# Four gate tiles in the attention heads' buffers, and the first output projection started with heads 0 to 3

## The chip, the core and the metric

The kernel runs on one core of one Trainium2 chip. The core has a matrix engine (TensorE, in the profile PE, with its weight loads listed as PEld), a vector engine (VectorE, DVE), an activation engine (ScalarE, ACT), a general engine (GpSimd, POOL) and a synchronising engine (SyncE, SP). In this kernel SP and ACT also issue the transfers (DMA) between the chip's memory and the core's on-chip memory (SBUF). Matmuls write into accumulators (PSUM), which here are eight banks of 128 x 512 f32: three called `acc`, two `s`, two `pt` and one `po`. The metric is the device time of one execution, in microseconds (us). The profiler's trace is of one execution; its span is a little shorter than the time of that execution.

## What is computed

The reference is two layers of a decoder trunk over 1024 rows of 1024 columns. Layer 0 is dilated window attention, layer 1 a gated linear recurrence, and each layer also attends to 256 memory rows. Around every mixer stands the same frame:

```
h = rms_norm(x, norm_gain[l])
cols = h @ w_in_a[j]
mix = dilated_mixer(cols[..., :3 * A_QKV], cos, sin, q_gain_a[j], k_gain_a[j])
gate = cols[..., 3 * A_QKV + MEM_WIDTH:]
...
y = jnp.concatenate([mix, mem_out], axis=-1) * jax.nn.silu(gate)
x = x + y @ w_out
```

`mix` has 1024 columns (8 heads of 128) and `mem_out` 512, so `y` has 1536 columns, and so has `gate`. The change lies at the seam between the last columns of layer 0's gate and layer 0's product `y @ w_out`.

## The kernel before

**Precision.** Every large product is done as three matmuls on f32r halves: both operands are split into a high and a low part, and high x high, high x low and low x high are added up in one accumulator. A weight piece (512 KB) is loaded into one of two `raw` buffers (line 195, issued by SP), ACT copies its high part (`wh`, line 166 through `copy`), DVE makes the low part (`wl`, line 212). `ahead(n)` prepares pieces up to n beyond the one in use, in the order of a list, `plan`; `rooms` says which pool each piece of the first output projection goes to.

**The order of the instructions** is not written out by hand: the program is traced, and a planner orders each engine's instructions by its own timeline of when their inputs will be ready; earlier program text has priority. Each engine then runs its list in that order. `tc.issue_after(ins)` makes the instructions traced inside it that run on the engine of `ins` stand behind `ins`; transfers issued by SP are not bound by it.

**The last stretch of layer 0.** `project_tiles` (line 229) computes 512 columns for eight tiles of 128 rows, two tiles at a time, 24 matmuls of 128 x 512 a tile (lines 252 to 254). The last attention group (`Q, g` = 1, 0: heads 4 to 7, window 128) projects k, v, q and attends tile by tile; `attend` for the last tile (line 922, with `merge`, line 901) is left over, and is run inside the gate projection that follows. It reads two `os` tiles of the pool `gs` (two buffers of 2 KB a partition), which lines 898 and 918 fill and use up, and its result goes to `o_scr` in the chip's memory (line 920).

**The gate projection** `gate_chunk(1, ...)` (line 504) computes the gate columns of heads 4 to 7. Its `each(m, ps)` runs once a tile: ACT takes tanh of the accumulator (line 500), DVE multiplies it on (line 501), after which the accumulator is free, and the tile is stored to `gate_scr` by a transfer that ACT issues (line 517). The tile buffer comes from the heads' pool `ap_` (name `qn`, two buffers) for m < 2 and from `gs` (`os`) for the rest. After tile 1 `between()` runs the last `attend`, closes the attention's pools (`s1`, `sa`) and opens, in `begin_out_a`, the pools of the output projection over their memory. After the tanh of tiles 3, 5 and 7 stand `ahead(4)`, `ahead(7)` and `ahead(10)`.

**The first output projection** `out_proj("out_a", ..., by_tile=True)` (line 570) multiplies `y` by `w_out_a`. The 1536 columns are taken in three blocks of 512, `b0` = 8 (the memory heads), 0 (heads 0 to 3) and 4 (heads 4 to 7), in the order of `FIRST`. A step is one `(b0, m)`: 24 matmuls (lines 632 to 634). Tiles 0 and 1 go block by block (steps (8,0), (8,1), (0,0), (0,1), (4,0), (4,1)), tiles 2 to 7 tile by tile. For every step `load_a` (line 716) loads the mixer's output `ol` and the gate `gt`, and `y_a` (line 741) multiplies them (line 744). For blocks 0 and 4 `transposed_split` follows: four transposes on PE (line 294), high part on ACT (line 166), low part on DVE (line 273). For block 8 the operands lie transposed in memory already: ACT copies the high part and DVE makes the low part (line 749), with no work on PE. `begin()` loads and makes the first two steps while the gate's last two tiles are projected; their `gt` lies in a buffer of its own (`spare`), later ones in `gs`. The two sums of tile 0 are in `acc`, those of tile 1 in `s`.

Of the kernel before, what the change touches and what calls it, by code (L numbers as in the profile page):

```python
# [46 lines left out]
NT = S // 128  # L47
# [8 lines left out]
SQB = 1  # L56
MGP = ((0,),(1,),(),())
MG1 = (2, 3)
FIRST = (8, 0, 4)
GATE_A, GATE_B = 9 * 1024 + 512, 3 * 1024 + 512  # L60


# [55 lines left out]
def trunk_kernel(ctx, tc, x, mem, pos, norm_gain, w_in_a, q_gain_a, k_gain_a, qk_gain_t, w_out_a,  # L118
# [10 lines left out]
    gs = ctx.enter_context(tc.tile_pool(name="gs", bufs=2))  # L129
# [99 lines left out]
    def ahead(n):  # L229

        while at_piece[1] < min(at_piece[0] + n, len(plan)):
            ready[at_piece[1]] = piece(*plan[at_piece[1]][1:])
            at_piece[1] += 1
# [201 lines left out]
    def rows(scr, g, m):  # L435

        r0, st = tile_rows(g, m)
        return scr[r0:r0 + 127 * st + 1:st, :]
# [45 lines left out]
    def sequence_rows(scr, m):  # L484


        return scr[m * 128:(m + 1) * 128].rearrange("(l e) c -> e l c", e=8)
# [11 lines left out]
    def twice_silu(dst, src):  # L499
        tanh = A.activation(dst, src, AF.Tanh, scale=0.5).ins  # L500
        V.scalar_tensor_tensor(dst, dst, 1.0, src, op0=OP.add, op1=OP.mult)  # L501
        return tanh

    def gate_chunk(c, by_residue, between=None, room=None, end=None):


        splits = {3: 4, 5: 7, 7: 10}

        def each(m, ps):
            pool, name = room if room and m < 2 else (gs, "os")  # L510
            sg = pool.tile([128, 4, 128], F32, name=name)[:].rearrange("p h d -> p (h d)")
            tanh = twice_silu(sg, ps)
            scr = gate_scr[:, c * 512:(c + 1) * 512]
            if by_residue:
                SQ.dma_start(rows(scr, 2, m), sg)
            else:
                SQ.dma_start(sequence_rows(scr, m), sg)
            if between and m == 1:
                between()
            if between and m in splits:  # L520

                with tc.issue_after(tanh):
                    ahead(splits[m])

        project_tiles(("gate", c), lhs_natural, each, end=end)
# [44 lines left out]
    def out_proj(key, load, load_x, y_T, x1, finish, pool, before, by_tile=False):  # L570

        steps = [(b0, m) for b0 in FIRST for m in range(NT)]
        if by_tile:
            steps = [s for s in steps if s[1] < 2] + [(b0, m) for m in range(2, NT) for b0 in FIRST]
        loaded, made, W, sums = {}, {}, {}, {}

        def weights(b0):  # L580
            p = take((key, b0), 4)
            W[b0] = [p[0:2], p[2:4]]

        def fetch(i):
            if i < len(steps):
                loaded[i], last = load(steps[i][1], steps[i][0])
                xm = i - XL if not by_tile and XL <= i < NT + XL else None
                if by_tile and steps[i][0] == FIRST[-1]:
                    xm = steps[i][1]
                if xm is not None:  # L590
                    with tc.issue_after(last.ins):
                        load_x(xm)

        def make(i):
            if i < len(steps):
                hi = pool.tile([128, 4, 128], F32R, name="yhi", bufs=LEAD + 1)
                lo = pool.tile([128, 4, 128], F32R, name="ylo", bufs=LEAD + 1)
                y_T(steps[i][1], steps[i][0], loaded.pop(i), hi, lo)
                made[i] = hi, lo

        def begin():
            for i in range(LEAD):
                fetch(i)
            for i in range(LEAD):
                make(i)
            before()

        def rest():
            fetch(LEAD)
            later = None  # L610
            for i, (b0, m) in enumerate(steps):
                if m == 0:
                    weights(b0)
                fetch(i + LEAD + 1)
                make(i + LEAD)
                if later:
                    later()
                    later = None
                hi, lo = made.pop(i)
                if m == 1 and not by_tile:  # L620
                    ahead(2)
                first, end = (b0 == FIRST[0], b0 == FIRST[-1]) if by_tile else (True, True)
                if first:
                    pool_, name = (pS, "s") if by_tile and m == 1 else (pp, "acc")
                    sums[m] = [pool_.tile([128, 512], F32, name=name) for _ in range(2)]
                pss = sums[m]
                last = i == len(steps) - 1 and key == "out_b"
                for kp, ch in ((0, 0), (1, 0), (0, 1), (1, 1)) if last else ((0, 0), (0, 1), (1, 0), (1, 1)):
                    wh, wl = W[b0][kp][ch]
                    for j in range(2):  # L630
                        k = 2 * kp + j
                        T.matmul(pss[ch][:], hi[:, k, :], wh[:, j, :], start=first and k == 0, stop=False)  # L632
                        T.matmul(pss[ch][:], hi[:, k, :], wl[:, j, :], start=False, stop=False)  # L633
                        T.matmul(pss[ch][:], lo[:, k, :], wh[:, j, :], start=False, stop=end and k == 3)  # L634
                    if by_tile and i == 1 and kp == 1:
                        ahead(7 + ch)
                    if m == NT - 1:
                        ahead(min(4, 2 + 2 * kp + ch) if by_tile else 3 + 2 * kp + ch)
                for ch, ps in enumerate(pss) if end else ():
                    xs = x1[m][:, ch * 512:(ch + 1) * 512]  # L640
                    V.tensor_tensor(xs, xs, ps[:], op=OP.add)
                if b0 == FIRST[-1]:
                    later = finish(m)
            if later:
                later()

        return begin, rest
# [18 lines left out]
            plan_chunk((n, Q, g), w_in_a, i * 3072 + g * 1024 + Q * 512, order=None if g else ROLLED)  # L666
    plan_chunk(("gate", 1), w_in_a, GATE_A + 512)

    def plan_out(key, w):
        for b0 in FIRST:  # L670
            for kp in (0, 2):
                for ch in range(2):
                    plan_chunk((key, b0), w, ch * 512, (b0 + kp) * 128, 256)

    plan_out("out_a", w_out_a)

    def plan_gate(i):
        plan_slice(("gate_b", i), w_in_b, GATE_B + i * 128)
# [16 lines left out]
            plan_chunk(("vb", 4), w_in_b, 2048 + 512)  # L695
    for i in gate_order[2]:
        plan_gate(i)
    plan_out("out_b", w_out_b)

    wide = ExitStack()  # L700


    s2, out_a = ExitStack(), []

    def begin_out_a(s2):
# [10 lines left out]
        def load_a(m, b0):  # L716
            r = slice(m * 128, (m + 1) * 128)
            o = op.tile([128, 512], F32, name="ol", bufs=2)

            if m < 2 and b0 == 8:  # L720
                if not spare:
                    spare.append(op.tile([128, D], F32, name="xn", bufs=1))
                gt = spare[0][:, m * 512:(m + 1) * 512]
            else:
                gt = gs.tile([128, 4, 128], F32, name="os")[:].rearrange("p h d -> p (h d)")
            if b0 == 8:
                for t, scr in ((o[:], om_scr), (gt, gatem_scr)):
                    last = LQ.dma_start(t.rearrange("p (k t) -> p k t", k=4), scr[:, r].rearrange("(k p) t -> p k t", p=128))
            else:
                LQ.dma_start(o[:], o_scr[r, 0, b0 * 128:b0 * 128 + 512])  # L730
                last = LQ.dma_start(gt, gate_scr[r, b0 * 128:b0 * 128 + 512])
            return (o, gt), last
# [31 lines left out]
    with ExitStack() as sa:  # L764
# [9 lines left out]
        with ExitStack() as s0:  # L774
# [3 lines left out]
            for m in range(NT):  # L778
                xt = ipool.tile([128, D], F32, name="xt")
                first = Y.dma_start(xt[:], rows(x, 2, m))  # L780
# [28 lines left out]
            rest, parts = 2.0 * math.pi, []  # L809
            while rest > 0:  # L810
                e = 2.0 ** (math.floor(math.log2(rest)) - 6)
                c = math.floor(rest / e) * e
# [46 lines left out]
            def spill_v(m, ps):  # L859
# [9 lines left out]
                    after=lambda hp: gate_mem(MG1[hp], mp[1], "qn"))  # L869
        sm.close()  # L870

        with ExitStack() as s1:
            vring = s1.enter_context(tc.tile_pool(name="vring", bufs=8))
            at_ = s1.enter_context(tc.tile_pool(name="attn", bufs=2))
            ap_ = s1.enter_context(tc.tile_pool(name="heads", bufs=2))
# [100 lines left out]
            for Q, g in group_order:  # L976
# [41 lines left out]
                end = (lambda i: ahead(min(3 + i, WR))) if final else None  # L1018
# [4 lines left out]
                project_tiles(("q", Q, g), lhs, each_q, order, end)  # L1023
                last = lambda: attend(Q, g, *waiting.pop(), kT, kl, vv)
                if final:
                    def between():
                        last()
                        s1.close()
                        sa.close()
                        out_a.append(begin_out_a(s2))  # L1030

                    def to_out(i):
                        if i == 0:
                            out_a[0][0]()

                    gate_chunk(1, False, between, (ap_, "qn"), to_out)
                else:
                    last()

# [4 lines left out]
    with ExitStack() as sb:  # L1044
# [257 lines left out]
        with ExitStack() as s7:  # L1302
# [25 lines left out]
            def load_x(m):  # L1328
                LQ.dma_start(x1[m], x1_scr[m * 128:(m + 1) * 128, :])
# [62 lines left out]
```

## Time and profile before

| | us |
|---|---|
| time, median of 3 runs (lowest to highest) | 2167.69 (2166.01 to 2167.97) |
| the profiled execution, its own time | 2167.61 |
| span of its trace | 2165.5 |
| TensorE busy in the span | 2137.0 |
| first matmul of gate tile 5 | 1247.73 |
| last matmul of the gate projection starts | 1265.56 |
| first matmul of the first output projection | 1265.79 |
| first matmul of its third step, (0,0) | 1290.76 |

Times inside the span count from its start. Three kinds of answers of the trace are used below. A list of waits has one line for each pair of a waiting operation and the one that released it, with the total, the count and the longest wait. A table of stretches has, for each, its length, every engine's busy time with its number of instructions, the granted clock of TensorE as a share of full speed, the share of time in which the DMA engines were busy, and GB/s. A timeline has the start, the length, the engine, the line, the operation, output and input, the shape and the count; in brackets stands how long the engine was idle before it and what it waited for. Matmuls overlap in it: what one costs in a stream is the distance between two starts.

### The profile page before, as it was taken

The page shows a single profiled execution, that of the slowest core. Times are in us where ns is not written, and L with a number is a line of the kernel's source. Part 1 is how long each engine was busy: PE and PEld are TensorE (multiplying, and loading weights), DVE is VectorE, ACT ScalarE, POOL GpSimd, SP SyncE. Part 2 cuts the span into 40 slices and gives each one's busy share as a digit, 9 for nine tenths or more (in the row PEclk, how much of TensorE's full clock was granted, in tenths as well). Part 3 has the DMA queues.
Part 4 walks back from the last instruction along what each step waited for, and adds up shares of the span by engine and source line. Part 5 has one row for each costly group of instructions (what it writes and reads, how often), then busy time and mean ns, then how long its engine had stood idle before and what let it go on. Part 6 is the DMA issues. An engine that isn't in the chain of part 4 may idle for free.

```text
span 2165.5 us, 29606 instructions
## 1 busy us (share of the span) xinstructions
PE 2137.0 (99%) x11273; PEld 1816.9 (84%) x11273; DVE 1060.8 (49%) x2403; ACT 730.0 (34%) x1507; POOL 370.9 (17%) x600
## 2 busy tenths in 40 slices
PE   8999999999999999999999979999999999999999
PEld 6888888888888888888888868888888888888887
DVE  6755323425414314425725744434557772776543
ACT  4545323424324324324423432233523222232211
POOL 1013212313403203302312000012200000000221
PEclk9999999999999999999999989999999999999999
DMA  6543211121222121122311475431211212113633
GB/s 200 140 138 72 46 51 56 51 69 41 60 67 56 48 64 47 33 69 58 107 47 52 126 231 163 136 106 44 88 35 50 64 54 59 49 50 98 233 119 115
DMA packets 181004, 183.49 MB, mean 85 GB/s; under 512 B 49008, under 2 KB 117760, under 8 KB 180864
## 3 DMA queue, kind: packets, MB, share of 16 engines
q1 hardware_dynamic: 116592, 138.48, 21.2%
q10 hardware_dynamic: 64272, 43.13, 7.0%
q8 instruction: 89, 1.46, 0.3%
q14 instruction: 51, 0.42, 0.1%
HBM read 138.45 MB, written 43.12 MB: 84 GB/s over the span
## 4 chain that ended last, share of the span: by engine, by line
PE 96%; DMA 2%; DVE 1%; ACT 0%; issue 0%; SPq 0%; POOL 0%; ACTq 0%; DVEq 0%
PE acc L252 16%; PE acc L253 16%; PE acc L254 16%; PE acc L536 5%; PE acc L537 5%; PE acc L538 5%; PE acc L632 4%; PE acc L633 4%; PE acc L634 4%; PE po L965 3%; PE pt L311 2%; PE s L946 2%; PE s L1147 1%; PE pt L1147 1%; PE pt L959 1%; DMA raw<-in_w_out_a_dram 1%
## 5 line engine op out<-in xcount | busy, mean ns | idle before, releaser
L252 PE MATMUL acc<-wh,hhi 128*128 128x512 f32 x1440 | 563.7, 395 | 4.6 <-DVE os L501 3.5
L254 PE MATMUL acc<-wh,hlo 128*128 128x512 f32 x1440 | 566.0, 395 | 0.0
L253 PE MATMUL acc<-wl,hhi 128*128 128x512 f32 x1440 | 565.7, 393 | 0.0
L175 POOL TENSOR_TENSOR rr<-rv,nhalf 128x4 f32<-128x4 f32 (+1 forms) x150 | 148.2, 988 | 1386.9 <-DVE rv L173 1361.2
L212 DVE TENSOR_TENSOR wl<-raw,wh 128x1024 fp32r<-128x1024 f32 x152 | 188.5, 1242 | 383.1 <-ACT wh L166 381.3
L252 PEld LDWEIGHTS acc<-wh,hhi 128*128 128x128 f32 x1440 | 271.5, 189 | 58.6 <-DVE os L501 3.7
L253 PEld LDWEIGHTS acc<-wl,hhi 128*128 128x128 f32 x1440 | 271.3, 188 | 53.6 <-DVE wl L212 0.4
L254 PEld LDWEIGHTS acc<-wh,hlo 128*128 128x128 f32 x1440 | 271.0, 188 | 53.5
L166 ACT ACTIVATE wh<-raw 128x1024 fp32r<-128x1024 f32 x152 | 160.9, 1059 | 192.3 <-PE acc L254 55.2
L538 PE MATMUL acc<-hhi,wl 128*128 128x512 f32 x512 | 203.8, 398 | 0.0
L537 PE MATMUL acc<-hlo,wh 128*128 128x512 f32 x512 | 203.6, 398 | 0.0
L536 PE MATMUL acc<-hhi,wh 128*128 128x512 f32 x512 | 202.9, 396 | 0.0
L302 DVE TENSOR_REDUCE ss<-sq 128x4 f32<-128x512 f32 x116 | 79.3, 684 | 144.1 <-ACT sq L300 144.0
L632 PE MATMUL acc<-wh,yhi 128*128 128x512 f32 x360 | 144.0, 402 | 4.6 <-DVE os L501 3.5
L633 PE MATMUL acc<-wl,yhi 128*128 128x512 f32 x360 | 142.3, 395 | 0.0
L634 PE MATMUL acc<-wh,ylo 128*128 128x512 f32 x360 | 139.9, 395 | 0.0
L300 ACT ACTIVATE sq<-acc 128x512 f32<-128x512 f32 x116 | 68.9, 594 | 181.1 <-PE acc L254 177.0
L305 DVE TENSOR_TENSOR qn<-acc,rr 128x512 f32<-128x512 f32 x116 | 79.7, 688 | 92.9 <-PE pt L311 50.6
L954 ACT ACTIVATE pa<-pa,st 128x128 f32<-128x128 f32 (+1 forms) x192 | 84.5, 442 | 99.4 <-DVE st L952 92.0
L537 PEld LDWEIGHTS acc<-hlo,wh 128*128 128x128 f32 x512 | 96.3, 188 | 17.9
L536 PEld LDWEIGHTS acc<-hhi,wh 128*128 128x128 f32 x512 | 96.3, 188 | 17.7
L538 PEld LDWEIGHTS acc<-hhi,wl 128*128 128x128 f32 x512 | 96.3, 188 | 17.5
(241 smaller groups left out, 3195.8 us busy)
## 6 DMA issues: line engine op xcount, KB each, us to landing
raw<-in_w_in_a_dram SPq DMA_DIRECT2D x88, 512.0 KB
raw<-in_w_in_b_dram SPq DMA_DIRECT2D x40, 512.0 KB
o_scr<-os ACTq DMA_DIRECT2D x48, 256.0 KB
raw<-in_w_mem_kv_dram SPq DMA_DIRECT2D x16, 512.0 KB
os<-o_scr SPq DMA_DIRECT2D x32, 256.0 KB
raw<-in_w_out_a_dram SPq DMA_DIRECT2D x12, 512.0 KB
raw<-in_w_out_b_dram SPq DMA_DIRECT2D x12, 512.0 KB
gt<-gateb_scr SPq DMA_DIRECT2D x24, 256.0 KB
```

What stands on the lines that cost most here:

```text
L166: A.activation(dst, src, AF.Copy)
L175: G.tensor_tensor(r[:], v[:], nhalf[:, :n], op=OP.pow)
L212: W_LO.tensor_tensor(lo[:], raw[:], hi[:].bitcast(F32), op=OP.subtract)
L252: T.matmul(ps, hi, wh[:, j, :], start=at == 0, stop=False)
L253: T.matmul(ps, hi, wl[:, j, :], start=False, stop=False)
L254: T.matmul(ps, lo, wh[:, j, :], start=False, stop=at == n - 1)
L536: T.matmul(to, wh[:, k, :], mh, start=k == 0, stop=False)
L537: T.matmul(to, wh[:, k, :], ml, start=False, stop=False)
L538: T.matmul(to, wl[:, k, :], mh, start=False, stop=k == 7)
L632: T.matmul(pss[ch][:], hi[:, k, :], wh[:, j, :], start=first and k == 0, stop=False)
L633: T.matmul(pss[ch][:], hi[:, k, :], wl[:, j, :], start=False, stop=False)
L634: T.matmul(pss[ch][:], lo[:, k, :], wh[:, j, :], start=False, stop=end and k == 3)
```

## The change

The first four gate tiles, not two, use the heads' buffers. The last attention step still stands after tile 1, but the closing of the attention's pools and the opening of the output projection's pools move behind tile 3 (`leave`). The preparation of weight pieces after tiles 3, 5 and 7 becomes `ahead(2)`, `ahead(6)`, `ahead(10)`. The first output projection takes its blocks in the order 0, 8, 4, so that the weight pieces are planned in that order, the first two steps are (0,0) and (0,1), and the spare gate buffer serves block 0. The second output projection keeps the order 8, 0, 4.

```diff
-FIRST = (8, 0, 4)
+FIRST, FIRST_A = (8, 0, 4), (0, 8, 4)
...
-    def gate_chunk(c, by_residue, between=None, room=None, end=None):
+    def gate_chunk(c, by_residue, between=None, after=None, room=None, end=None):
...
-        splits = {3: 4, 5: 7, 7: 10}
+        splits = {3: 2, 5: 6, 7: 10}
...
-            pool, name = room if room and m < 2 else (gs, "os")
+            pool, name = room if room and m < 4 else (gs, "os")
...
             if between and m == 1:
                 between()
-            if between and m in splits:
+            if after and m == 3:
+                after()
+            if after and m in splits:
...
-        steps = [(b0, m) for b0 in FIRST for m in range(NT)]
+        parts = FIRST_A if by_tile else FIRST
+        steps = [(b0, m) for b0 in parts for m in range(NT)]
         if by_tile:
-            steps = [s for s in steps if s[1] < 2] + [(b0, m) for m in range(2, NT) for b0 in FIRST]
+            steps = [s for s in steps if s[1] < 2] + [(b0, m) for m in range(2, NT) for b0 in parts]
...
-    plan_out("out_a", w_out_a)
+    plan_out("out_a", w_out_a, FIRST_A)
...
-            if m < 2 and b0 == 8:
+            if m < 2 and b0 == FIRST_A[0]:
...
-                    def between():
-                        last()
+                    def leave():
                         s1.close()
                         sa.close()
                         out_a.append(begin_out_a(s2))
...
-                    gate_chunk(1, False, between, (ap_, "qn"), to_out)
+                    gate_chunk(1, False, last, leave, (ap_, "qn"), to_out)
```

The other lines of the diff replace `FIRST[0]` and `FIRST[-1]` by `parts[0]` and `parts[-1]` in `out_proj`, and hand `FIRST` to the second plan.

More of the change, by code (lines that the diff above doesn't have):

```diff
@@ L587, in fetch @@
                 xm = i - XL if not by_tile and XL <= i < NT + XL else None
-                if by_tile and steps[i][0] == FIRST[-1]:
+                if by_tile and steps[i][0] == parts[-1]:
                     xm = steps[i][1]
@@ L621, in rest @@
                     ahead(2)
-                first, end = (b0 == FIRST[0], b0 == FIRST[-1]) if by_tile else (True, True)
+                first, end = (b0 == parts[0], b0 == parts[-1]) if by_tile else (True, True)
                 if first:
@@ L641, in rest @@
                     V.tensor_tensor(xs, xs, ps[:], op=OP.add)
-                if b0 == FIRST[-1]:
+                if b0 == parts[-1]:
                     later = finish(m)
@@ L667, in trunk_kernel, with plan_out @@
     plan_chunk(("gate", 1), w_in_a, GATE_A + 512)
-    def plan_out(key, w):
-        for b0 in FIRST:
+    def plan_out(key, w, parts):
+        for b0 in parts:
             for kp in (0, 2):
@@ L697, in trunk_kernel @@
         plan_gate(i)
-    plan_out("out_b", w_out_b)
+    plan_out("out_b", w_out_b, FIRST)
     wide = ExitStack()
```

## The prediction

> **What bounds the kernel now.** I read the page first, then TensorE's list of waits over the whole span.
>
> ```profile
> span 2165.5 us, 29606 instructions
> ...
> PE 2137.0 (99%) x11273; PEld 1816.9 (84%) x11273; DVE 1060.8 (49%) x2403; ACT 730.0 (34%) x1507; POOL 370.9 (17%) x600
> ```
> ```profile
> PE pt L294 <- DVE xn L286: 8.5, 1, 8.5
> PE pt L294 <- DVE ol L744: 5.3, 2, 4.7
> PE acc L252 <- DVE os L501: 3.5, 1, 3.5
> PE acc L632 <- DVE os L501: 3.5, 1, 3.5
> PE acc L632 <- ACT yhi L166: 1.0, 1, 1.0
> ```
>
> TensorE is idle for 2165.5 - 2137.0 = 28.5 us. The 8.5 is the start of the kernel. The other four lines, 5.3 + 3.5 + 3.5 + 1.0 = 13.3 us, are all at the seam that the change edits; so this seam is nearly all that such a change can win. The timeline of TensorE puts them in order, and the table of stretches shows what each does to the clock:
>
> ```profile
> 1247.73 0.50 PE L252 MATMUL acc<-wh,hhi 128*128 128x512 f32 x1 [3.51 <-DVE os L501]
> ...
> 1252.16 0.39 PE L252 MATMUL acc<-wh,hhi 128*128 128x512 f32 x1
> ...
> 1265.56 0.39 PE L254 MATMUL acc<-wh,hlo 128*128 128x512 f32 x1
> ...
> 1275.13 0.50 PE L632 MATMUL acc<-wh,yhi 128*128 128x512 f32 x1 [3.51 <-DVE os L501]
> ...
> 1286.90 1.11 PE L294 MATMUL pt<-ident,ol 128*128 128x128 f32 x4 [4.68 <-DVE ol L744]
> ...
> 1290.76 0.79 PE L632 MATMUL acc<-wh,yhi 128*128 128x512 f32 x1 [1.00 <-ACT yhi L166]
> ```
> ```profile
> 1247.70:1265.80 18.10, 18.07 (x73) 14.77 (x74) 9.82 (x11) 8.05 (x10) 0.00 (x0) 0.91 0.74 226
> ...
> 1275.10:1282.20 7.10, 7.07 (x23) 5.38 (x23) 3.02 (x3) 2.12 (x2) 0.00 (x0) 0.76 0.70 195
> ...
> 1290.80:1296.30 5.50, 5.50 (x13) 4.30 (x14) 2.51 (x4) 1.45 (x2) 0.00 (x0) 0.52 1.02 347
> 1296.30:1440.00 143.70, 143.63 (x692) 119.32 (x691) 68.18 (x96) 39.30 (x59) 4.88 (x8) 1.00 0.48 154
> ```
>
> Three gaps are to be seen, each followed by a stretch of low granted clock (0.91, 0.76 and 0.52 on average); behind 1296.30 TensorE is full at clock 1.00. The whole seam runs from 1247.73 - 3.51 = 1244.22 to 1296.30, 52.1 us. From 1252.16 to 1265.56 lie 59 matmuls, so a warm one takes 0.227 us.
>
> ```profile
> L252 PE MATMUL acc<-wh,hhi 128*128 128x512 f32 x24 | 10.2, 423 | 3.5 <-DVE os L501 3.5
> ```
> ```profile
> 1321.12 0.87 PE pt L294 x8
> ```
>
> Between 1244.2 and 1265.8 line 252 runs 24 times (the list of groups for that stretch), and lines 253 and 254 with it: 72 matmuls, three gate tiles, so tile 5's first matmul is the one that waits at 1247.73. Warm work in the seam: 72 gate matmuls, two steps of 24, and the 13 behind 1290.8, 133 x 0.227 = 30.2, plus eight transposes at 0.87 (a warm eight at 1321.12), 31.0 us. So 52.1 - 31.0 = **21.1 us** of the seam are not work: 13.3 of waits, some 6 of low clock (18.1 x 0.09 + 7.1 x 0.24 + 5.5 x 0.48 = 6.0), the rest cold transposes.
>
> **Part by part: tiles 2 and 3 in the heads' buffers.** The rows of ACT, DVE and the chain that matter:
>
> ```profile
> 1235.29 0.39 PE L254 MATMUL acc<-wh,hlo 128*128 128x512 f32 x1
> ```
> ```profile
> 1221.14 0.59 ACTq L517 DMA_DIRECT2D gate_scr<-qn  x1
> ...
> 1246.35 0.60 ACT L500 ACTIVATE os<-acc 128x512 f32<-128x512 f32 x1 [0.96 <-DVE os L918]
> ...
> 1257.68 1.14 ACT L166 ACTIVATE yhi<-ol 128x512 fp32r<-128x512 f32 x1 [4.90 <-DMA ol<-om_scr]
> 1258.73 1.05 ACT L166 ACTIVATE wh<-raw 128x1024 fp32r<-128x1024 f32 x1
> 1259.67 0.58 ACT L500 ACTIVATE os<-acc 128x512 f32<-128x512 f32 x1
> ...
> 1272.16 1.06 ACT L166 ACTIVATE wh<-raw 128x1024 fp32r<-128x1024 f32 x1 [0.96 <-DMA raw<-in_w_out_a_dram]
> 1273.12 1.07 ACT L500 ACTIVATE os<-acc 128x512 f32<-128x512 f32 x2
> ```
> ```profile
> 1244.65 2.19 DVE L918 SCALAR_TENSOR_TENSOR os<-os,mw 128x128 f32<-128x128 f32 x8 [3.37 <-ACT os L915]
> ```
>
> Tiles 2 and 3 are summed by about 1235, since the next tile's 24 matmuls had all run before the gap; but tile 2's tanh comes at 1246.35, because its `os` buffer is held by the last merge (line 918, to 1246.84). In the heads' buffers it waits only for an earlier gate store (issued at 1221.14), long landed. TensorE then goes on from 1244.22 without the first gap: **3.5 + 1.6** us go. What is late next: the wait for the merge passes to tile 4's tanh, whose accumulator TensorE wants only for the third tile from there, 24 matmuls or 5.4 us later (1249.7); free by then (1246.9 + 0.6 + 0.7 = 1248.2). I cost it at nothing; without that cover it is the old 3.5. The gate projection would end, unhindered, at 1244.2 + 16.3 = 1260.5.
>
> **Fewer pieces after tile 3.** `ahead(2)` leaves six pieces before tile 6's tanh where seven stood; at 1272.16 the seventh held up tiles 6 and 7 on ACT (sums ready at 1265.8, tanh at 1273.12). With tile 3's tanh some 10 us sooner the pieces behind it start sooner too, and that block should be gone: the second gap, **3.5 + 1.7**, goes. Bound from the other side: if one piece still stands before it with a load as late, up to 3.6 us stay.
>
> **Block 0 first.** The first two steps now need eight transposes inside the gate's last matmuls, where block 8 needed none on TensorE. The transposes themselves only change places (0.9 us, in the 31.0). Their data:
>
> ```profile
> 1246.88 3.98 DMA o_scr<-os
> ...
> 1276.81 7.35 DMA gate_scr<-os
> ...
> 1284.65 4.49 DMA raw<-in_w_out_a_dram
> ```
> ```profile
> 1251.02 0.37 SPq L728 DMA_DIRECT2D ol<-om_scr  x1
> ...
> 1282.63 1.93 SPq L731 DMA_DIRECT2D os<-gate_scr  x2
> ```
> ```profile
> 1256.91 0.69 DVE L744 TENSOR_TENSOR ol<-ol,xn 128x512 f32<-128x512 f32 x1 [3.40 <-DMA ol<-om_scr]
> ...
> 1286.15 0.69 DVE L744 TENSOR_TENSOR ol<-ol,os 128x512 f32<-128x512 f32 x1 [5.22 <-DMA os<-gate_scr]
> ```
>
> The first load of the new pools is issued at 1251.02, when the last merge's store has landed (1246.88 + 3.98); nothing in the change moves that merge. Load to product took 5.9 us there (1251.02 to 1256.91, with weights in the air) and 3.5 at 1282.63; for block 0, with two weight pieces already in, I take the middle, 4.7. The product ends at 1251.0 + 4.7 + 0.7 = 1256.4. When does TensorE come to the transposes? It takes its list in order, and the planner placed them by its own timeline. Before, ACT's list has the high part of step 1 (1257.68) and a weight copy (1.05) ahead of tile 5's tanh (1259.67): the planner believed both done before tile 5 was summed, 24 warm matmuls behind tile 2's line 501 (1247.7 + 5.4 = 1253.1), hence the product by 1252.0. It believes transfers shorter than they are. So the transposes will stand near 1252.0, with some 38 of the 72 matmuls queued behind, and hold them 1256.4 - 1252.0 = **4.4 us**, a new wait. It is longer than the 3.51 that lowered the clock, so 1.7 more, and 0.4 for the second step's product. Bounds: 0 (placed late enough) and 1.2 + 1.9 more with the 5.9 load and a position before tile 5's end. The gate then ends at 1260.5 + 0.9 + 6.5 = 1267.9, 2 us later than now, with the transposes done.
>
> The clock rule: the Trainium skill (TensorE: Matmul & The Clock Gate, What's actually happening) says that a free-running window of about 3.4 us, found idle, halves the clock. By it a wait of 4.4 us need not hold a whole window; without the loss the time would be an estimated 1.7 us lower. The two 3.51 gaps here both lost it. The same page (Part 4: PE-mode transpose) says that transposes don't count as busy in the same way, which speaks against putting them behind a stall; it would add about their own 0.9 us of low clock. The 0.52 behind the transposes of 1286.90 agrees.
>
> **The third step** is now (8,0), without transposes. Its gate goes into the buffer of gate tile 6, as before. Counted from the end X of the gate: tanh 0.6, line 501 0.7, issue 0.7, store 5.8 (issued until 1276.8; the load behind it starts at 1282.63), load 3.5, product 0.7, copy 1.14: X + 13.3. TensorE has 48 matmuls, 10.9 us, so it waits **2.5 us**, too short for me to count a clock loss. Bounds: 0.6 with a store of 3.98, and about 6.3 + 1.7 with 7.35 and a load of 5.9. Its first two weight pieces (4.5 us a load, 4.49 above) should be copied by X. Strided copies (1.14) replace 0.6 ones on ACT later, under full TensorE.
>
> Sum: 21.1 - 6.5 - 2.5 = 12.1 us less, if what follows stays full as it is after 1296.30. From 2167.6 (the profiled execution, 0.1 under the median): **2155.5 us**.
>
> **Rivals.** *In time*: the planner places the transposes late enough; only the 2.5 remain, 2149.0. For it: ACT and DVE are freer; against it: the order on ACT above. *The wait returns*: the transposes cost 4.4 + 3.1, and the third step 8.0, since a weight piece on SP stands behind a gate load that waits for a store (1284.65 before) and ACT's copy of it ahead of the operand's: 21.1 - 7.5 - 1.7 - 8.0 = 3.9, 2163.7. *No gain*: tile 4's tanh takes the first gap over (3.5 + 1.6) on top of this: 2168.8, or about the same. *Slower*: the order 0, 8, 4 also holds for tiles 2 to 7, where block 0's transposes now come at each tile's change, just after block 4, and its loads share `gs` with it. If TensorE waits there 3 us six times, 18 - 12.1 = 5.9 us are lost: 2173.5. It decides from 2.0 us a tile. Against it: the lead of two steps is 10.9 us, loads took 3.5 to 5.9, and after 1296.30 nothing waited.
>
> **Chances.** Forecast 0.45 (2152.5 to 2159.5); in time 0.2; the wait returns 0.18, half of it beyond 0.2% (4.3 us, about what a measurement of this kernel can tell from no change); no gain 0.09; slower 0.08. Faster 0.45 + 0.2 + 0.09 = 0.74, same 0.09 + 0.09 = 0.18, slower 0.08. The range 2148.0 to 2165.5 leaves out slower, no gain and a little of the time under "in time".
>
> **What would show it.** Right: line 252 no longer waits for line 501; tanh of tile 2 near 1236; a wait of line 294 for line 744 inside the gate, 3 to 6 us; tiles 6 and 7's tanh right behind their sums; a wait of 1 to 4 us of line 632 at the third step. Wrong: no wait at the transposes (in time), one of over 7, a remaining line 501 wait, or waits of line 294 spread over tiles 2 to 7.

## The result, and the profile after

The changed kernel takes 2156.4 us (median of 4 runs, 2154.47 to 2156.85) against 2167.83 us before (4 runs, 2166.01 to 2169.87): the ratio is 0.9945, with a 95% interval from 0.9928 to 0.9963. The forecast was 2155.5. Line numbers behind line 504 are higher by two or three in the changed kernel: the matmuls of the output projection are lines 635 to 637, the product of `y_a` is 747, the last merge 921.

The page of the changed kernel, span and engines, then TensorE's list of waits over its whole span (total, count, longest):

```profile
span 2153.7 us, 29607 instructions
...
PE 2134.1 (99%) x11273; PEld 1815.0 (84%) x11273; DVE 1060.0 (49%) x2403; ACT 730.2 (34%) x1507; POOL 370.8 (17%) x600
```
```profile
PE pt L294 <- DVE xn L286: 9.3, 2, 8.6
PE pt L294 <- DVE ol L747: 2.6, 1, 2.6
...
PE acc L635 <- ACT yhi L166: 0.5, 1, 0.5
...
PE pt L294 <- issue: 0.5, 1, 0.5
```

Both waits for line 501 are gone, and so is the 4.7 us of the third step. Of the seam there remain 2.6 + 0.5 at the transposes. Behind it, at 1307.12 and 1323.74, stand two short waits that were not there before: 0.7 (the second of the two waits for `xn`, at a tile change of the projection) and 0.5 at an operand. Together this is 4.3 us in place of 13.3. The timeline of TensorE at the end of the gate, and the stretches around it (length, busy time and count of PE, PEld, DVE, ACT, POOL, granted clock, DMA share, GB/s):

```profile
1260.76 0.39 PE L254 MATMUL acc<-wh,hlo 128*128 128x512 f32 x1
1261.60 0.63 PE L294 MATMUL pt<-ident,ol 128*128 128x128 f32 x4 [0.46 <-issue]
...
1262.53 0.40 PE L254 MATMUL acc<-wh,hlo 128*128 128x512 f32 x1
1265.48 1.11 PE L294 MATMUL pt<-ident,ol 128*128 128x128 f32 x4 [2.55 <-DVE ol L747]
1266.70 0.80 PE L635 MATMUL acc<-wh,yhi 128*128 128x512 f32 x1
```
```profile
1247.30:1261.10 13.80, 13.80 (x62) 11.12 (x60) 6.31 (x13) 4.23 (x8) 0.00 (x0) 1.00 0.55 175
1261.10:1266.70 5.60, 2.49 (x12) 1.59 (x12) 3.33 (x5) 3.09 (x5) 0.00 (x0) 0.80 0.63 213
1266.70:1271.90 5.20, 5.20 (x13) 4.12 (x14) 3.74 (x5) 2.13 (x3) 0.00 (x0) 0.56 0.93 288
1271.90:1290.00 18.10, 18.10 (x83) 15.01 (x82) 7.75 (x9) 6.28 (x6) 0.00 (x0) 1.00 0.88 314
```

The gate runs through at full clock to its last three matmuls; the second step's transposes stand behind a wait of 2.55 us, and 5.2 us at a mean clock of 0.56 follow, which cost an estimated 5.2 x 0.44 = 2.3 us. From 1271.9 on TensorE is full, through the third step, which begins at 1279.84 (1290.76 before).

Where the time went is read best between two marks outside the seam: the last score matmuls of attention, and the first sigmoid of layer 1. Before, then after (first and last start stand behind the durations):

```profile
L941 PE MATMUL s<-kT,qT x64: 274/282/367, 993.6 to 1231.3; 128*128 128x256 f32 x64
...
L1110 ACT ACTIVATE ff<-acc x16: 577/586/600, 1579.8 to 1946.4; 128x512 f32<-128x512 f32 x16
```
```profile
L944 PE MATMUL s<-kT,qT x64: 275/283/367, 994.8 to 1232.5; 128*128 128x256 f32 x64
...
L1112 ACT ACTIVATE ff<-acc x16: 577/586/600, 1567.9 to 1934.5; 128x512 f32<-128x512 f32 x16
```

From mark to mark it is 348.5 us before and 335.4 after: the seam gave **13.1 us**. The profiled execution after was 1.2 us late already at the first mark, and is 11.8 shorter in all.

### The profile page after: what moved, and what is told of

It reads as the page before. It is cut to its first block, busy times and chain, and to the rows that moved or that the text cites. A ratio compares the mean times of both kernels' runs of the same rounds, so it can differ in the third digit from the quotient of the medians.

```text
span 2153.7 us, 29607 instructions
## 1 busy us (share of the span) xinstructions
PE 2134.1 (99%) x11273; PEld 1815.0 (84%) x11273; DVE 1060.0 (49%) x2403; ACT 730.2 (34%) x1507; POOL 370.8 (17%) x600
## 4 chain that ended last, share of the span: by engine, by line
PE 95%; DMA 2%; DVE 2%; issue 1%; ACT 1%; SPq 0%; POOL 0%; ACTq 0%; DVEq 0%
PE acc L252 16%; PE acc L253 16%; PE acc L254 16%; PE acc L538 5%; PE acc L539 5%; PE acc L540 5%; PE acc L635 4%; PE acc L636 4%; PE acc L637 4%; PE po L968 3%; PE pt L311 2%; PE s L949 2%; PE pt L1149 1%; PE s L1149 1%; PE pt L962 1%; PE pt L294 1%
```

## The experiments

Each kernel below is a variant of the changed one (or of the one before, in the last). The table has the median, the ratio to the kernel before with its interval, the stretch between the two marks, the waits of TensorE between 1225 and 1450 us, and the granted clock from 1240 to 1300 us, these three from the profiled execution. The ratio is to runs of the kernel before that were measured beside each group (medians 2166.6 to 2167.8), so it compares better than the medians do. A profiled execution can lie off its median: 1.9 us below it for the last row, 3.0 above it for the pieces 4, 7, 10.

| kernel | us | ratio (95%) | marks | waits | clock |
|---|---|---|---|---|---|
| before | 2167.8 | 1 | 348.5 | 13.3 | 0.86 |
| changed | 2156.4 | 0.9945 (0.9928 to 0.9963) | 335.4 | 4.3 | 0.94 |
| tiles alone | 2158.2 | 0.9957 (0.9945 to 0.9970) | 338.4 | 7.0 | 0.94 |
| order alone | 2165.5 | 0.9992 (0.9983 to 1.0001) | 344.6 | 12.4 | 0.91 |
| pieces 2, 6, 10 alone | 2166.8 | 0.9999 (0.9990 to 1.0008) | 347.4 | 12.3 | 0.86 |
| changed, pieces 4, 7, 10 | 2156.9 | 0.9951 (0.9937 to 0.9964) | 338.2 | 6.6 | 0.94 |
| changed, pieces 2, 4, 10 | 2152.2 | 0.9930 (0.9917 to 0.9942) | 333.0 | 2.7 | 1.00 |
| the same, order 8, 0, 4 | 2159.2 | 0.9961 (0.9947 to 0.9974) | 338.5 | 7.7 | 0.97 |
| changed, pieces 4, 4, 10 | 2153.7 | 0.9941 (0.9929 to 0.9954) | 333.1 | 2.8 | 1.00 |
| changed, pieces 2, 2, 10 | 2161.2 | 0.9972 (0.9960 to 0.9983) | 342.2 | 8.7 | 0.94 |
| changed, order for tiles 0, 1 only | 2154.6 | 0.9942 (0.9929 to 0.9954) | 333.7 | 3.2 | 0.97 |
| pieces 2, 4, 10, order for tiles 0, 1 only | 2152.6 | 0.9932 (0.9920 to 0.9945) | 330.8 | 2.1 | 1.00 |

**The gate tiles alone**

```diff
-FIRST, FIRST_A = (8, 0, 4), (0, 8, 4)
+FIRST, FIRST_A = (8, 0, 4), (8, 0, 4)
...
-        splits = {3: 2, 5: 6, 7: 10}
+        splits = {3: 4, 5: 7, 7: 10}
```

> Gate tiles 2 and 3 in the heads' buffers alone; order 8, 0, 4 and the pieces 4, 7, 10 as before. Theory (each gap has its own cause): the wait of the gate's first line for line 501 (3.5 us and 1.6 of low clock) goes, the other two stay: about 5 us less than before, 2162 to 2163. Rival (one chain: weight pieces, paced by their loads, hold up tile 6's tanh, whatever TensorE gains ahead of it): the gate ends 5 us sooner and the next gaps grow by as much; within 1.5 us of before, 2166 to 2169.

The pools of the output projection open behind tile 3 here too, as in the changed kernel. Measured: 2158.2, 9.2 us under the kernel before, measured beside it (2167.46). Neither case: both waits for line 501 went, not one. What remains in the seam, in its list of waits from 1225 to 1450, besides one of 0.2:

```profile
PE acc L635 <- ACT yhi L166: 4.9, 2, 3.4
PE pt L294 <- DVE ol L747: 1.9, 2, 1.1
```

The 3.4 is at the first step: its operand waits for block 8's first loads. The second gap needed no part of its own; it follows the first. ACT's list, with seven pieces as before, shows how: the third and fourth piece are copied at 1244.97 and 1246.78, since tile 3's tanh stands at 1237.96 (1247.57 before).

```profile
1237.96 0.58 ACT L500 ACTIVATE qn<-acc 128x512 f32<-128x512 f32 x1
...
1244.97 1.06 ACT L166 ACTIVATE wh<-raw 128x1024 fp32r<-128x1024 f32 x1 [3.51 <-DMA raw<-in_w_out_a_dram]
1246.78 1.06 ACT L166 ACTIVATE wh<-raw 128x1024 fp32r<-128x1024 f32 x1 [0.75 <-DMA raw<-in_w_out_a_dram]
...
1265.75 0.58 ACT L500 ACTIVATE os<-acc 128x512 f32<-128x512 f32 x1
```

Two 512 KB pieces are so out of the way before the new pools open, and the tanh of tile 6, 1273.12 before, begins at 1265.75, that of tile 7 at 1268.82.

**The order alone**

```diff
-        splits = {3: 2, 5: 6, 7: 10}
+        splits = {3: 4, 5: 7, 7: 10}
...
-            pool, name = room if room and m < 4 else (gs, "os")
+            pool, name = room if room and m < 2 else (gs, "os")
...
-            if after and m == 3:
+            if after and m == 1:
```

> Order 0, 8, 4 alone; gate tiles 2 to 7 in the two old buffers, pieces 4, 7, 10. Theory: the first two gaps (line 501, 3.5 us each) stay, the third shrinks by the transposes (about 2 us) unless the transposes wait in the gate: 2164 to 2168. Rival (the order is what brings the gain): 2157 to 2160.

Measured: 2165.5, 2.0 us less, its interval just reaching no change. TensorE's waits from 1225 to 1450:

```profile
PE acc L635 <- ACT yhi L166: 5.6, 2, 5.1
PE acc L252 <- DVE os L501: 3.5, 1, 3.5
PE pt L294 <- DVE ol L747: 2.2, 2, 2.1
PE pt L294 <- issue: 1.1, 1, 1.1
```

The first gap is there, new waits of 1.14 and 2.06 us stand at the transposes within the gate, and the third step waits 5.05 us for its operand. So the time is the theory's, but not all of its parts: the second wait for line 501 is not there. The tanh of tiles 6 and 7 is as late as before (1273.67), but the transposes' waits and the low clock hold the gate's last matmul back to 1270.71 (1265.56 before), and TensorE comes to the accumulator only when it is free.

**The pieces alone**, on the kernel before

```diff
-        splits = {3: 4, 5: 7, 7: 10}
+        splits = {3: 2, 5: 6, 7: 10}
```

> The kernel before with pieces 2, 6, 10 alone. Theory of the prediction (the seventh piece ahead of tile 6's tanh makes the second gap): 3 to 5 us less than before, 2162 to 2164. Rival (the pieces are paced by loads that start at 1251 whatever their number; the tiles' buffers are what moved them): within 1.5 us of before.

Measured: 2166.8 against 2166.9. The rival holds: one piece fewer ahead of tile 6's tanh moves nothing. Tiles 6 and 7 have their tanh at 1274.96, and the second gap is no shorter than it was (TensorE's waits of this kernel):

```profile
PE acc L632 <- DVE os L501: 4.0, 1, 4.0
PE acc L252 <- DVE os L501: 3.6, 1, 3.6
```

**The changed kernel with the old pieces, and with fewer**

```diff
-        splits = {3: 2, 5: 6, 7: 10}
+        splits = {3: 4, 5: 7, 7: 10}
```

> The changed kernel with the pieces after tiles 3, 5, 7 as before (4, 7, 10). Theory: a seventh piece stands before tile 6's tanh again, its accumulator is late and the second gap comes back in part: 3 to 5 us more than the changed kernel, 2159 to 2162. Rival (once tile 3's tanh is early the numbers don't matter): within 1.5 us of the changed kernel, 2155 to 2158.

```diff
-        splits = {3: 2, 5: 6, 7: 10}
+        splits = {3: 2, 5: 4, 7: 10}
```

> The changed kernel with pieces 2, 4, 10: the fifth and sixth come after tile 7's tanh instead of after tile 5's. Theory (the second transposes' product stands on VectorE behind the low part of the fifth piece, whose load lands at 1262.5): the wait of 2.6 us before the transposes and the low clock behind it (2.3) shrink by half or more: 2152 to 2154.5. Rival (the product waits for its own loads): the wait stays, 2156 to 2157. Second rival: block 8's pieces are now late and the third step waits for them by 3 us or more: 2156 to 2160.

Measured: 2156.9 (2155.91 to 2159.84) with the old pieces, the rival's; 2152.2 (2151.26 to 2152.92) with 2, 4, 10, the theory's. The runs don't overlap, 4.6 us lie between the medians. VectorE's list of the changed kernel, and below it that with 2, 4, 10:

```profile
1263.60 1.23 DVE L212 TENSOR_TENSOR wl<-raw,wh 128x1024 fp32r<-128x1024 f32 x1 [2.10 <-ACT wh L166]
1264.74 0.69 DVE L747 TENSOR_TENSOR ol<-ol,xn 128x512 f32<-128x512 f32 x1
```
```profile
1258.70 0.69 DVE L747 TENSOR_TENSOR ol<-ol,xn 128x512 f32<-128x512 f32 x1 [4.57 <-DMA ol<-o_scr]
1260.55 0.69 DVE L747 TENSOR_TENSOR ol<-ol,xn 128x512 f32<-128x512 f32 x1 [1.16 <-DMA xn<-gate_scr]
```

In the changed kernel the second step's product starts right behind the fifth piece's low part, which waits for ACT's copy, and that for a load issued at 1256.53 that takes 5.96 us. Without the piece the product runs as soon as its own loads are in, 1.85 us behind the first, and TensorE's wait is 0.38 in place of 2.55, with no low clock behind it (1.00 from 1240 to 1300). The order on VectorE is only a part of this. By the semaphore records in the trace, the changed kernel's second product had its last load in at 1263.73, 1.0 us before it started. Most of the rest is that load itself: issued 1.84 us behind the first step's first load and 6.27 us on its way, against 1.32 and 5.65 with 2, 4, 10. The edit also moves the sixth piece, and no run parts these effects. The third step then waits 0.79 and 0.40 us: what stood hidden behind the longer wait.

**That version with the old order**

```diff
-FIRST, FIRST_A = (8, 0, 4), (0, 8, 4)
+FIRST, FIRST_A = (8, 0, 4), (8, 0, 4)
...
-        splits = {3: 2, 5: 6, 7: 10}
+        splits = {3: 2, 5: 4, 7: 10}
```

> Gate tiles in the heads' buffers and pieces 2, 4, 10, with the old order 8, 0, 4. Against the same with order 0, 8, 4 (2152.2). Theory (the order matters by itself: block 8's first loads land some 2 us later, and the third step gets its transposes back): a wait at the first step of 1 to 3 us and some 2 us at the third, 2154 to 2158. Rival (with the pieces out of the way the order is worth nothing): 2151 to 2153.5.

Measured: 2159.2, 7.0 us over 2, 4, 10 with the new order (the kernel before took 2166.59 beside this one and 2167.46 beside that): the theory holds, by more than it said. First step 0.6 and 0.4 us, third and fourth 1.7, 1.2 and 1.4, and a low clock behind them. The order is worth 2 us alone, 1.4 on top of the tiles with pieces 4, 7, 10 (2158.2 and 2156.9), and some 7 here. So its worth hangs on the pieces, and theirs on it: with the old order, 2, 4, 10 is no faster than 4, 7, 10 (2159.2 and 2158.2).

**Pieces 4, 4, 10 and 2, 2, 10**

```diff
-        splits = {3: 2, 5: 6, 7: 10}
+        splits = {3: 4, 5: 4, 7: 10}
```

> The changed kernel with pieces 4, 4, 10: four pieces right behind tile 3's tanh, none behind tile 5's. Theory (what counts is that the fifth and sixth piece stand behind tile 7's tanh): as with 2, 4, 10, 2151 to 2153.5. Rival (the third and fourth piece on ScalarE's list ahead of tile 4's tanh hold up a store or a tanh while they wait for their loads): 2 us or more above that, 2154 to 2157.

Measured: 2153.7 (2153.49 to 2157.09), between the two cases; its trace has the same stretch between the marks as 2, 4, 10 (333.1 and 333.0). Where the third and fourth piece stand matters little.

```diff
-        splits = {3: 2, 5: 6, 7: 10}
+        splits = {3: 2, 5: 2, 7: 10}
```

> The changed kernel with pieces 2, 2, 10: only two pieces ahead of tile 7's tanh. Theory (the first step needs four pieces within 5.5 us of its start, and the third and fourth are now copied behind tile 7's tanh, from about 1263.5 on): the first step waits 1 to 3 us for them and the clock falls or not, 2152 to 2157. Rival (a raw buffer's load is early enough whatever the place of the copy): 2151 to 2153.

Measured: 2161.2, over the range of the theory. The first step does not wait; but the third to the eighth piece are copied 10 to 13 us later than with 2, 4, 10, and the third step's first matmul is held up by the first copy of its weights. The longest wait, 3.87 us, is for the seventh piece, copied at 1285.04, and the low clock is behind it (TensorE's timeline):

```profile
1274.45 0.51 PE L635 MATMUL acc<-wh,yhi 128*128 128x512 f32 x1 [0.93 <-ACT wh L166]
1276.33 0.50 PE L636 MATMUL acc<-wl,yhi 128*128 128x512 f32 x1 [1.38 <-DVE wl L212]
1286.15 0.80 PE L635 MATMUL acc<-wh,yhi 128*128 128x512 f32 x1 [3.87 <-ACT wh L166]
```

So of the counts tried four is the best: with six pieces ahead of tile 7's tanh the products wait, with two the weights do, and with 2, 4, 10 no single wait is over 0.8 us.

**The new order for the first two tiles only**

```diff
-            steps = [s for s in steps if s[1] < 2] + [(b0, m) for m in range(2, NT) for b0 in parts]
+            steps = [s for s in steps if s[1] < 2] + [(b0, m) for m in range(2, NT) for b0 in FIRST]
...
-                first, end = (b0 == parts[0], b0 == parts[-1]) if by_tile else (True, True)
+                first, end = (b0 == (parts if m < 2 else FIRST)[0], b0 == parts[-1]) if by_tile else (True, True)
```

> The changed kernel with the order 0, 8, 4 for tiles 0 and 1 only; tiles 2 to 7 take 8, 0, 4 as before. Theory (the order of the later tiles costs nothing, behind the seam TensorE is full either way): within 1.5 us of the changed kernel, 2155 to 2158. Rival (the order costs a little at every tile change): 1.5 to 4 us less, 2152 to 2155.

Measured: 2154.6, 1.8 us under the changed kernel, with intervals that overlap widely (0.9929 to 0.9954 and 0.9928 to 0.9963). The stretch between the marks is 1.7 shorter; the 0.7 and the 0.5 us behind the seam are gone from the list of waits. But most of the 1.7 is not theirs. Both kernels have nearly the same wait at the gate's end (2.45 and 2.55 us), and here the clock is back at 1.00 some 2.0 us behind the next matmul, where the changed kernel takes 4.6. Against 0.227 us for a warm matmul, the low clock there costs 1.1 us here and 2.3 in the changed kernel. So the rival is not shown, neither by the times nor by the trace.

**Both together**

> Pieces 2, 4, 10 and the order 0, 8, 4 for tiles 0 and 1 only, together. Theory (two separate gains: 4.2 from the pieces, some 1.8 from the later order): 2149.5 to 2151.5. Rival (with the seam already full the later order is worth nothing that can be measured): 2151.5 to 2153.

This joins the two edits, pieces 2, 4, 10 and the later tiles' old order. Measured: 2152.6 (2150.68 to 2153.91), no better than the pieces alone by the times, though its trace, of the fastest of its five executions, has the shortest stretch between the marks, 330.8. The two can't be told apart by these runs; either beats the changed kernel by some 4 us.

## Why the prediction was right, and where it was not

The forecast of 12.1 us less met 11.4 in the medians and 13.1 at the seam. Its sign and size came from one reading that held: that 21.1 us of the seam were waits and low clock, that they all lay there, and that what came behind was full. Its terms held less well, so that the number came out so near is in part luck. Of the signs that it named, one came as said: line 252 no longer waits for line 501. Tile 2's tanh came 8 us ahead of the 1236 it gave, tile 7's began 4.3 us behind its sum (1262.93) instead of right behind, the wait at the transposes was under its 3 to 6 us, and the third step had none.

- **The first gap** (3.5 + 1.6): right. Tile 2's tanh comes at 1227.84, tile 3's at 1238.24, and line 252 no longer waits in the seam. The cover that I named held: tile 4's tanh takes over the wait for the merge, and nobody waits for it.
- **The second gap** (3.5 + 1.7): it went, but for another reason. The step "fewer pieces after tile 3" gave the gain to the numbers 2, 6, 10; alone they give 0.1 us of 2166.9, and the changed kernel without them is 0.5 us slower by the medians, with intervals that overlap. The tiles alone close it; by ACT's list it is because tile 3's early tanh lets two pieces through before the pools open. The sentence that the pieces behind tile 3 start sooner had the cause; the count of pieces was no part of it.
- **"Nothing in the change moves that merge"**: wrong. TensorE, with its gate matmuls free to run, reached the last 16 matmuls of attention at 1245.36 in place of 1242.27, and the first load of the new pools was issued at 1255.62, not 1251.02. Of these 4.6 us, 1.2 were there before the seam. TensorE had gate work meanwhile, so it cost nothing by itself, but the loads for the transposes came that much later.
- **The transposes' wait**: there as forecast, of another make. Forecast: 4.4 us in the middle of the gate for the first step's loads, and 0.4 for the second's. Measured: 0.46 for the first, 3 matmuls before the gate's end, and 2.55 for the second, behind its last. The planner did place the first about where the data came; for the second, the load came late and the fifth weight piece stood ahead of the product on VectorE's list, which by the trace is 1.0 of the 2.55 us. I had looked for a late load on the operand's own path, and not at what stood ahead of it on VectorE.
- **The low clock behind it**: 1.7 forecast, 2.3 measured. The prediction counted no loss for a wait of 2.5 us; here one of 2.55 had it. Nor does the 0.52 behind the transposes of 1286.90 speak against transposes, as the prediction has it: the clock had fallen by 1285.84, ahead of them (the mean of 1285 to 1286 is 0.92, of the next stretch 0.50).
- **The third step's wait** of 2.5: none. The chain from the gate's end was longer than the 13.3 that I wrote (its terms add up to 13.1): 15.5, from 1262.8 to 1278.3, the end of the operand's copy. But TensorE came later still, 17.0 us behind the gate's end, since the transposes' wait and the low clock lay in between. I had put that wait ahead of the gate's end, where it delays both sides alike. With the wait taken away by the pieces 2, 4, 10, some 1.2 us of it show (0.79 and 0.40).
- **The sum**: 9.0 us left over by forecast (6.5 at the transposes, 2.5 at the third step); by measurement 21.1 - 13.1 = 8.0. Of these, 0.5 + 2.6 + 2.3 lie at the transposes and 0.7 + 0.5 behind the seam; the other 1.4 are not placed.
- **The rival that ended slower** (the order of the later tiles): its mechanism leaves traces, 0.7 and 0.5 us in all, not 3 us at each of six tiles.

## What to carry to other kernels

When an engine that is full elsewhere has a cluster of gaps at a seam between two stages, find the first buffer that is held: here one pair of buffers of 2 KB a partition, moved, closed two gaps and gave 9.2 of 11.4 us, and the count of the pieces that looked guilty of the second gap was worth nothing alone. Each engine takes its list in order, so for every step that is moved look at what stands ahead of it on each engine that it uses, and among the loads, weight preparation above all: taking two pieces of 512 KB from ahead of one product and its operand gave some 4 us. And test such counts again after the change, on both sides: 2, 4, 10 beat 2, 6, 10, while 2, 2, 10 lost 5 us against 2, 6, 10. Two changes can also need each other, as the order and these counts did, so a part that is worth 1 or 2 us alone is not yet to be thrown out.

## What the runs showed of the hardware

The clock of TensorE fell behind waits shorter than the 3.51 us that the trace before had shown. In the changed kernel one of 2.55 us was enough; the table of stretches, in steps of 1 us for TensorE alone, shows the fall within the wait, and the return some 4.6 us behind the first matmul (1266.70). Below it two steps of the kernel with the new order for two tiles only, whose wait is 2.45 us:

```profile
1264.00:1265.00 1.00, 0.00 (x0) 0.74 0.13 51
1265.00:1266.00 1.00, 0.52 (x3) 0.50 0.28 16
...
1271.00:1272.00 1.00, 1.00 (x5) 0.85 0.64 229
```
```profile
1263.00:1264.00 1.00, 0.03 (x1) 0.89 0.02 8
...
1267.00:1268.00 1.00, 1.00 (x5) 0.91 1.04 281
```

The clock in such a table is 1.00 or 0.50 but for the step in which it changes, so a mean of 0.74 puts the fall at 1264.48, and 0.85 the return at 1271.30: 6.8 us at half clock. In the other kernel it is 3.4 us, from 1263.78 to 1267.18. Read so, the twelve traces have fourteen falls between 1238 and 1300 us, and each lasts 3.4, 6.8 or 10.2 us (the longest is the third of the kernel before, from 1285.84). So, at half clock, a fall costs an estimated 1.7 us for each 3.4 us in which TensorE has work throughout, and nearly the same wait can bring 3.4 us of it or 6.8. What decides between them is not shown.

In the kernel with pieces 2, 4, 10 and the old order no wait of the seam was longer than 1.75 us, and it fell all the same, behind this row of short ones:

```profile
1273.60 0.66 PE L294 MATMUL pt<-ident,ol 128*128 128x128 f32 x4 [1.75 <-DVE ol L747]
...
1275.01 0.39 PE L637 MATMUL s<-wh,ylo 128*128 128x512 f32 x1
1276.58 0.66 PE L294 MATMUL pt<-ident,ol 128*128 128x128 f32 x4 [1.18 <-DVE ol L747]
1278.59 0.50 PE L635 MATMUL acc<-wh,yhi 128*128 128x512 f32 x1 [1.36 <-ACT yhi L166]
```
```profile
1278.00:1279.00 1.00, 0.41 (x2) 0.99 0.84 305
1279.00:1280.00 1.00, 1.00 (x4) 0.50 1.00 358
```

Between the matmul of 1275.01 and that of 1278.59 lie only four transposes. The Trainium skill (TensorE: Matmul & The Clock Gate, What's actually happening) puts the fall at an idle window of about 3.4 us; its Part 4 says that transposes don't count as busy in the same way. By both together, the 3.2 us from the end of the one matmul to the other would be nearly such a window. In the changed kernel the 3.4 us ahead of the fall at 1264.48 are not wholly idle: they hold three gate matmuls (1261.98 to 1262.93). Two traces show waits after which the clock stayed at 1.00: with the tiles alone 2.89 us between two matmuls (1280.98 to 1283.87) held only four transposes, and with pieces 2, 2, 10 waits of 0.93 and 1.38 us stood with one matmul between them and no transposes. So it is not shown that the transposes are what makes the short waits count.
